# Delta tiles as pairs of 512 and 256 columns, with a gate tile behind every second one

## The chip, the cores and the metric

The kernel runs on one core of one Trainium2 chip. The metric is the device time of one execution in microseconds (us); the time before is the median of three runs.

## The reference, cut to what matters

Two transformer blocks run one after the other on 256 tokens of width 2048, all in float32. Block 1 normalises x and projects it with one wide matrix `w_in`. The parts of that projection are used as follows:

```
att_qkv, dn_qkv, dn_z, dn_beta, dn_alpha, gate_a, gate_b = split(xn @ w_in)
y_a = neighbourhood_attention(aq, ak, av)                 # 8 heads of 128
q, k, v = split(silu(conv5(dn_qkv)))                      # depthwise, over tokens
y_b = rmsnorm(gated_delta(q, k, v, ...)) * silu(dn_z)     # 8 heads of 128, both directions
mixed = sigmoid(gate_a) * (y_a @ w_proj_a) + sigmoid(gate_b) * (y_b @ w_proj_b)
h = x + mixed @ w_out
h = h + square(relu(rmsnorm(h) @ w_mlp_up)) @ w_mlp_down
```

The gated delta rule solves, per head and chunk of tokens, a unit lower triangular system, in both directions of time. Block 2 (another attention, a gated linear attention and a convolved feed-forward layer) is not touched by the change.

## The kernel before

**Products of one tile.** A weight tile is 2048 x 128 values: 16 slices (k) of 128 x 128. To keep float32 accuracy every operand is split in a high part of type fp32r and a rest: ACT casts the raw weights to `hi` (`split_weights`, L314), DVE subtracts to get `lo` (L233, called at L315). The activations `xa` (tiles A0 to A3) hold high and low part of one k side by side, 256 columns each. `tile_mm` (L368) works one tile off into `acc`, one PSUM bank of 2 x 256 float32 columns, of which there are three. `products` (L338) has two forms. With `one=False` each k has a product of 512 columns (hi by both parts of x, into both halves of acc) and one of 256 columns (lo by the high part, into the first half). The two halves are added later by `total` (L443): a copy on ACT (L446) and an addition on DVE (L448). With `one=True` each k has three products of 256 columns, all into the first half, and nothing is left to add.

**Weights.** `plan` is the list of all weight tiles in their order of use, `want` (L290) appends to it. `emit_split` (L322) takes the next one: SP fetches it into one of three raw buffers, ACT and DVE split it into two pieces of 8 slices, of which four pairs of buffers exist, so two tiles.

**Delta tiles.** `heads_project` (L688) with `dn_post` (L720) works off 12 tiles of four heads: 4 of q, 4 of k, 4 of v. For each, `conv_silu` (L674) scales acc by the tokens' norm into `pre`, convolves (one ACT pass, four DVE passes) and gates with a tanh. The first two tiles of all are computed side by side by `two_mm` (L427) and wait in `spare`; for these alone `two` is true and the halves are added. The other 22 (10 in the first group of heads, 12 in the second) use `one=True`.

**Gate tiles.** `gates` (L1019) works off tiles of gate_b (to the DRAM tensor `gbd`) or gate_a (`gad`): `one=False`, `total`, a multiplication, a tanh.

**Background work and its planner.** After a group's 12 delta tiles, `block1_mix` appends `dn_chain` (L731) to the list `bg`: norms, decays and products per head (the steps with `qku` and `kkm`), four transposes on DVE (L813), 31 substitution steps of two DVE instructions each (L819, L821), then copies on ACT, small products on PE that complete the inverses, and `dn_head` (L876) per head. The chain is a generator: each `yield` names a cost in us, or, negative, a number of slices to hold. `pump` (L477) runs after every fourth slice of a product; it adds `rate` / 4 to `credit` (at most 2.2) and lets the first generator of `bg` run while the credit is positive, at most two steps a call. `rate` is `DNR` = 0.7 in a delta tile and `SPARE` = 2.2 in a gate tile and in an attention tile. `finish` (L508) issues all that is left of a generator at once, and its costs are taken off the credit all the same.

**The order of stages.** `block1_mix` (L1028) issues: the delta tiles of group 0; 16 tiles of gate_b and 4 of gate_a (`GA`), beside which chain 0 runs; the delta tiles of group 1; the last 12 tiles of gate_a, beside which chain 1 begins; then, for the attention, 8 tiles (q and k of heads 0 to 3) and one wide product (v), `finish(dn[1])`, 8 tiles (heads 4 to 7), and the chains `na_chain` (L995) of the two groups. The delta q and k of group 1 lie in the tiles M2 and M3, and the attention's q and k of its second group go to M2 and M3 again, so these wait until chain 1 has read them. Last come 8 tiles of z, then `finish()`, then w_proj_a. Group, chain and head numbers below count from 0.

**What sets the order on an engine.** Within this text order the framework places an instruction on its engine's queue as soon as its operands and buffers are there and nothing earlier in the text is ready; the engine's queue itself is fixed when the program is built.

Of the kernel before, what the change touches and what calls it, by code (L numbers as in the profile page):

```python
# [18 lines left out]
KT = D // P  # L19
# [4 lines left out]
SPARE = 2.2  # L24
# [7 lines left out]
GA = 4  # L32
# [142 lines left out]
class Net:  # L175
# [544 lines left out]
    def dn_post(self, j, h, qk, v):  # L720
        v, stage = v
        self.rate = DNR
        two = bool(self.spare)
        acc = self.tile_mm(self.xa, one=True)
        y, th = self.conv_silu(acc, 8 * j + h, two)
        if j < 2:
            self.stt(qk[:, j], th, 1.0, y, ALU.add, ALU.mult)
        else:
            self.stt(stage, th, 1.0, y, ALU.add, ALU.mult)

    def dn_chain(self, g, qk, vt, stage):  # L731
        nc = self.nc
# [285 lines left out]

    def gates(self, d, a, b):  # L1019
        st = self.b4("B3", F32, (P, 8, T))  # L1020
        self.rate = SPARE
        for m in range(a, b):
            z = self.evac(self.tile_mm(self.xa), "cy")
            self.act(st[:, m % 8], z, AF.Tanh, scale=0.5)
            if m % 4 == 3:
                self.nc.gpsimd.dma_start(d[:, m - 3:m + 1], st[:, m % 8 - 3:m % 8 + 1])

    def block1_mix(self):  # L1028
        nc = self.nc
        heads = lambda g, b, n: [self.want("w_in", b + 8 * j + 4 * g, 4) for j in range(n)]  # L1030
        heads(0, 16, 3)
        self.want("w_in", 64, 16)
        self.want("w_in", 48, GA)
        heads(1, 16, 3)
        self.want("w_in", 48 + GA, 16 - GA)
        heads(0, 0, 2)
        self.want_chunk(self.I["w_in_v"])
        heads(1, 0, 2)
        self.want("w_in", 40, 8)
        self.want("w_proj_a", 0, 16, 0, 8)  # L1040
        self.want("w_proj_b", 0, 16, 0, 8)
        self.want_wide("w_out")

        gbd = self.dram.tile([P, KT, T], F32, name="gbd")
        gad = self.dram.tile([P, KT, T], F32, name="gad")
        accs = self.setup()
        self.first_two(self.xa)
        vs = self.b4("H1", F32, (P, 2, 512))
        gr = self.tmp([P, 2, 32], "rr", bufs=1)
        for t in range(2):  # L1050
            r = self.rT[:, t:t + 1]
            self.act(gr[:, t], accs[t][:, 0:32], AF.Copy, scale=r)
            self.act(vs[:, t, 0:240], accs[t][:, 32:272], AF.Copy, scale=r)
            self.act(vs[:, t, 240:512], accs[2 + t][:, 0:272], AF.Copy, scale=r)
        self.vd = [self.dram.tile([P, 2, 512], F32, name="vd%d" % i) for i in range(2)]
        nc.gpsimd.dma_start(self.vd[0], vs)
        self.bg.append(self.dn_gates(gr))
        self.oT = [self.b4("H0")]
        dn = []
        for g in range(2):  # L1060
            stage = self.b4("H1" if g else "H3")
            qk, vt = self.heads_project(g, self.dn_post, stage)
            dn.append(self.dn_chain(g, qk, vt, stage))
            self.bg.append(dn[-1])
            if g == 0:
                self.gates(gbd, 0, KT)
            self.gates(gad, GA * g, KT if g else GA)
        ya = []
        na = []
        for g in range(2):  # L1070
            self.finish(dn[g])
            qk, vt = self.heads_project(g, self.na_post)
            if g == 0:
                tag = "B3"
            else:
                self.finish(dn[1])
                tag = "B2"
            self.ya = ya = ya + self.acts(tag)
            na.append(self.na_chain(g, qk, vt))
            self.bg.append(na[-1])  # L1080
        self.finish(dn[1])
        yb = self.acts("B0", "B1")

        self.rate = 1.2
        for h in range(8):
            z = self.evac(self.tile_mm(self.xa), "cy")
            th = self.tmp([P, T], "th")
            self.act(th, z, AF.Tanh, scale=0.5)
            self.stt(z, th, 1.0, z, ALU.add, ALU.mult)
            o = self.oT[h // 4][:, h % 4]  # L1090
            self.tt(z, o, z, ALU.mult)
            self.split(yb[h], z)
        self.finish()
        ma = [self.b4("M%d" % i) for i in range(4)]
        for i in range(4):
            nc.gpsimd.dma_start(ma[i], gad[:, 4 * i:4 * i + 4])
        mb = [self.b4("H%d" % i) for i in range(4)]
        for i in range(4):
            nc.gpsimd.dma_start(mb[i], gbd[:, 4 * i:4 * i + 4])
        for m in range(KT):  # L1100
            a = ma[m // 4][:, m % 4]
            self.stt(a, a, 1.0, self.total(self.tile_mm(self.ya)), ALU.add, ALU.mult)
        mx = self.actsA()
        for m in range(KT):
            b = mb[m // 4][:, m % 4]
            self.stt(b, b, 1.0, self.total(self.tile_mm(yb, m == 15)), ALU.add, ALU.mult)
            self.tt(b, b, ma[m // 4][:, m % 4], ALU.add)
            self.split(mx[m], b)
        return mx
# [480 lines left out]
```

## Time and profile before

| | us |
|---|---|
| median of 3 runs (2564.48 to 2567.22) | 2566.35 |
| the profiled execution, whole | 2567.14 |
| its span, first to last instruction | 2565.3 |
| PE busy | 2549.0 (99%) |
| PE weight loads busy | 2210.4 (86%) |
| DVE busy | 1762.0 (69%) |
| ACT busy | 1368.6 (53%) |

A matmul record overlaps the next one, since products are pipelined, so the distance between two starts is what one costs; a busy PE is not a PE at its peak. The granted clock of TensorE is 1.00 (2.4 GHz) in every stretch that is used below.

### The profile page before, as it was taken

Reading aid. Unit: us, or ns where it says so; the run is one execution under the profiler, and the core shown is the slowest. Engines: PE = TensorE matmul, PEld = TensorE weight load, DVE = VectorE, ACT = ScalarE, POOL = GpSimd, SP = SyncE. Lnnn points to the kernel's source line nnn. Section 1 sums busy time; section 2 is a strip of 40 time slices with the busy share of each in tenths; the row PEclk is TensorE's granted clock in tenths of the full one; section 3 lists DMA queues with packets and bytes.
Section 4 is the critical chain, followed back from the end, with each engine's and each line's share of the span. In section 5 each row is a group of like instructions: output and inputs, shape, how many; then the busy total and the mean of one; then the engine's idle time right before and its main releaser. Section 6 shows DMA issues by size and latency. Waiting matters only on the chain.

```text
span 2565.3 us, 37124 instructions
## 1 busy us (share of the span) xinstructions
PE 2549.0 (99%) x14386; PEld 2210.4 (86%) x14386; DVE 1762.0 (69%) x2953; ACT 1368.6 (53%) x2277; POOL 49.6 (2%) x102
## 2 busy tenths in 40 slices
PE   8999999999999999999999999999999999999999
PEld 8989988888888888888888888888888888888887
DVE  7887879477856556556556677676688658875884
ACT  6555664665555435445445566655555445543553
POOL 0010000000000000000000000000000000000000
PEclk9999999999999999999999999999999999999999
DMA  7565455455755555555555564445555555555554
GB/s 266 184 214 205 165 197 198 149 200 188 255 182 190 188 196 190 189 196 188 191 196 186 189 216 162 147 165 183 182 194 188 190 197 186 192 195 187 193 190 155
DMA packets 76832, 488.82 MB, mean 191 GB/s; under 512 B 9080, under 2 KB 9368, under 8 KB 24433
## 3 DMA queue, kind: packets, MB, share of 16 engines
q1 hardware_dynamic: 68112, 457.34, 50.2%
q0 software_dynamic: 8256, 28.55, 3.4%
q8 instruction: 113, 1.85, 0.3%
q10 hardware_dynamic: 288, 0.57, 0.1%
q14 instruction: 63, 0.51, 0.1%
HBM read 476.95 MB, written 9.47 MB: 190 GB/s over the span
## 4 chain that ended last, share of the span: by engine, by line
PE 82%; DVE 2%; issue 1%; ACT 1%; DMA 0%; POOL 0%; ACTq 0%; POOLq 0%
PE acc L248 62%; PE s L248 20%; PE s L251 1%; DVE lo L233 0%; DVE rsu L233 0%; DMA rB<-rd 0%; DMA A<-in_c_dram 0%; ACT hi L314 0%; ACT big L245 0%; DVE rsr L236 0%; DVE M L233 0%; DVE sc L236 0%; DVE B L236 0%; ACT B L832 0%; DVE ea L233 0%
## 5 line engine op out<-in xcount | busy, mean ns | idle before, releaser
L233 DVE TENSOR_TENSOR lo<-raw,hi 128x1024 fp32r<-128x1024 f32 (+3 forms) x880 | 1060.3, 1206 | 693.8 <-ACT hi L314 690.7
L314 ACT CAST hi<-raw 128x1024 fp32r<-128x1024 f32 (+3 forms) x880 | 912.1, 1037 | 1014.2 <-PE acc L248 652.6
L248 PE MATMUL acc<-B,hi 128*128 128x512 f32 x2944 | 1028.6, 393 | 0.0
L248 PE MATMUL acc<-B,lo 128*128 128x256 f32 x2944 | 825.7, 280 | 0.0
L248 PEld LDWEIGHTS acc<-B,hi 128*128 128x128 f32 x2944 | 551.1, 187 | 121.6
L248 PEld LDWEIGHTS acc<-B,lo 128*128 128x128 f32 x2944 | 556.4, 189 | 0.3
L248 PE MATMUL acc<-A,hi 128*128 128x512 f32 (+1 forms) x1632 | 463.3, 352 | 0.0
L248 PE MATMUL s<-hi,A 128*128 128x512 f32 (+1 forms) x1280 | 384.2, 381 | 7.6 <-ACT hi L314 7.6
L248 PE MATMUL acc<-hi,A 128*128 128x512 f32 x1152 | 362.7, 390 | 0.0
L248 PE MATMUL acc<-A,lo 128*128 128x256 f32 x1280 | 359.5, 281 | 0.0
L248 PEld LDWEIGHTS acc<-A,hi 128*128 128x128 f32 x1632 | 283.6, 189 | 38.9 <-issue 0.2
L248 PEld LDWEIGHTS s<-hi,A 128*128 128x128 f32 x1280 | 235.6, 189 | 52.8 <-ACT hi L314 7.6
L248 PEld LDWEIGHTS acc<-hi,A 128*128 128x128 f32 x1152 | 216.2, 188 | 44.9
L248 PEld LDWEIGHTS acc<-A,lo 128*128 128x128 f32 x1280 | 242.5, 189 | 0.8
L248 PE MATMUL s<-lo,A 128*128 128x512 f32 (+1 forms) x640 | 238.6, 381 | 0.7 <-DVE lo L233 0.6
L248 PE MATMUL acc<-lo,A 128*128 128x512 f32 x576 | 224.2, 389 | 0.1
L248 PEld LDWEIGHTS s<-lo,A 128*128 128x128 f32 x640 | 118.7, 189 | 23.7 <-DVE lo L233 1.3
L236 DVE SCALAR_TENSOR_TENSOR cy<-pre,par,cy 128x256 f32<-128x256 f32 x272 | 130.5, 482 | 5.4 <-ACT cy L245 0.6
L248 PEld LDWEIGHTS acc<-lo,A 128*128 128x128 f32 x576 | 108.1, 188 | 22.6 <-DVE lo L233 0.5
L233 DVE TENSOR_TENSOR ea<-acc,eb 128x256 f32<-128x256 f32 x258 | 107.7, 418 | 0.8 <-ACT eb L446 0.8
L446 ACT COPY eb<-acc 128x256 f32<-128x256 f32 x258 | 93.4, 363 | 0.0
L248 PE MATMUL acc<-hi,B 128*128 128x512 f32 (+2 forms) x192 | 68.7, 369 | 0.0
(284 smaller groups left out, 1647.2 us busy)
## 6 DMA issues: line engine op xcount, KB each, us to landing
raw<-in_w_in_dram SPq DMA_DIRECT2D x112, 1024.0 KB, 4.8
raw<-in_w_up_dram SPq DMA_DIRECT2D x88, 1024.0 KB, 4.8
raw<-in_w_mlp_up_dram SPq DMA_DIRECT2D x64, 1024.0 KB, 4.8
raw<-in_w_mlp_down_dram SPq DMA_DIRECT2D x64, 1024.0 KB, 4.6
raw<-in_w_down_dram SPq DMA_DIRECT2D x44, 1024.0 KB, 4.6
raw<-in_w_out_dram SPq DMA_DIRECT2D x32, 1024.0 KB, 4.7
raw<-in_w_proj_a_dram SPq DMA_DIRECT2D x16, 512.0 KB, 3.5
raw<-in_w_proj_b_dram SPq DMA_DIRECT2D x16, 512.0 KB, 3.4
```

Of the source, the lines that this page charges most:

```text
L233: return (eng or self.nc.vector).tensor_tensor(out=out, in0=a, in1=b, op=op).ins
L236: self.nc.vector.scalar_tensor_tensor(out=out, in0=a, scalar=s, in1=b, op0=op0, op1=op1)
L248: self.nc.tensor.matmul(out, lhsT, rhs, start=start, stop=stop)
L251: self.nc.tensor.transpose(out, a, self.ident[0:a.shape[0], 0:a.shape[0]])
L314: self.nc.scalar.copy(hi, w)
L446: self.nc.scalar.copy(t, acc[0:np_, 1])
```

## The change

Delta tiles take the other form of product (512 and 256 columns for each slice) and add their halves as all others do. `gates` becomes a generator that works off one tile a step; `dn_post` takes a step of it behind every second delta tile. Six gate tiles of a group so lie between its delta tiles, and the other ten follow behind them, after the group's chain has been appended. Group 0 now has all 16 tiles of gate_b, group 1 all 16 of gate_a. The list of weights is put in the same order.

```diff
     def dn_post(self, j, h, qk, v):
         v, stage = v
         self.rate = DNR
-        two = bool(self.spare)
-        acc = self.tile_mm(self.xa, one=True)
-        y, th = self.conv_silu(acc, 8 * j + h, two)
+        acc = self.tile_mm(self.xa)
+        y, th = self.conv_silu(acc, 8 * j + h, True)
         if j < 2:
             self.stt(qk[:, j], th, 1.0, y, ALU.add, ALU.mult)
         else:
             self.stt(stage, th, 1.0, y, ALU.add, ALU.mult)
+        if h % 2 == 1:
+            next(self.between)
...
     def gates(self, d, a, b):
         st = self.b4("B3", F32, (P, 8, T))
-        self.rate = SPARE
         for m in range(a, b):
+            self.rate = SPARE
             z = self.evac(self.tile_mm(self.xa), "cy")
             self.act(st[:, m % 8], z, AF.Tanh, scale=0.5)
             if m % 4 == 3:
                 self.nc.gpsimd.dma_start(d[:, m - 3:m + 1], st[:, m % 8 - 3:m % 8 + 1])
+            yield
...
-        heads(0, 16, 3)
-        self.want("w_in", 64, 16)
-        self.want("w_in", 48, GA)
-        heads(1, 16, 3)
-        self.want("w_in", 48 + GA, 16 - GA)
+        for g, m in ((0, 64), (1, 48)):
+            for j in range(6):
+                self.want("w_in", 16 + 8 * (j // 2) + 4 * g + 2 * (j % 2), 2)
+                self.want("w_in", m + j, 1)
+            self.want("w_in", m + 6, 10)
...
             stage = self.b4("H1" if g else "H3")
+            self.between = self.gates(gad if g else gbd, 0, KT)
             qk, vt = self.heads_project(g, self.dn_post, stage)
             dn.append(self.dn_chain(g, qk, vt, stage))
             self.bg.append(dn[-1])
-            if g == 0:
-                self.gates(gbd, 0, KT)
-            self.gates(gad, GA * g, KT if g else GA)
+            for i in self.between:
+                pass
```

## Rows read from the trace of the kernel before

**Rows 1.** Page, part 1: busy us, share and instructions of each engine.

```profile
PE 2549.0 (99%) x14386; PEld 2210.4 (86%) x14386; DVE 1762.0 (69%) x2953; ACT 1368.6 (53%) x2277; POOL 49.6 (2%) x102
```

**Rows 2.** Page, part 4: the chain that ended last, by engine.

```profile
PE 82%; DVE 2%; issue 1%; ACT 1%; DMA 0%; POOL 0%; ACTq 0%; POOLq 0%
```

**Rows 3.** Windows: us, busy us (instructions) of engines; clock, DMA share, GB/s.

```profile
47.00:108.30 61.30, 61.18 (x509) 60.44 (x508) 56.01 (x128) 36.12 (x64) 2.71 (x5) 1.00 0.62 207
...
397.00:441.40 44.40, 44.40 (x258) 38.83 (x257) 42.70 (x96) 18.45 (x25) 0.68 (x2) 1.00 0.55 197
441.40:472.60 31.20, 31.07 (x322) 24.74 (x321) 14.97 (x16) 19.99 (x35) 1.53 (x4) 1.00 0.48 170
472.60:598.00 125.40, 124.74 (x749) 109.47 (x747) 84.93 (x212) 81.77 (x193) 9.04 (x16) 1.00 0.49 171
```

**Rows 4.** Timeline, PE: start, us; two successive delta tiles' first products.

```profile
59.36 0.40 PE L248 MATMUL acc<-A,hi 128*128 128x256 f32 x2
...
65.12 0.40 PE L248 MATMUL acc<-A,hi 128*128 128x256 f32 x2
```

**Rows 5.** Timeline, PE: first products of two pairs of successive gate tiles.

```profile
129.68 0.40 PE L248 MATMUL acc<-A,hi 128*128 128x512 f32 x1
...
135.32 0.40 PE L248 MATMUL acc<-A,hi 128*128 128x512 f32 x1
...
183.79 0.39 PE L248 MATMUL acc<-A,hi 128*128 128x512 f32 x1
...
189.34 0.39 PE L248 MATMUL acc<-A,hi 128*128 128x512 f32 x1
```

**Rows 6.** Page, part 5: group, count; busy us, mean ns; idle before, releaser.

```profile
L233 DVE TENSOR_TENSOR lo<-raw,hi 128x1024 fp32r<-128x1024 f32 (+3 forms) x880 | 1060.3, 1206 | 693.8 <-ACT hi L314 690.7
...
L236 DVE SCALAR_TENSOR_TENSOR cy<-pre,par,cy 128x256 f32<-128x256 f32 x272 | 130.5, 482 | 5.4 <-ACT cy L245 0.6
L233 DVE TENSOR_TENSOR ea<-acc,eb 128x256 f32<-128x256 f32 x258 | 107.7, 418 | 0.8 <-ACT eb L446 0.8
L446 ACT COPY eb<-acc 128x256 f32<-128x256 f32 x258 | 93.4, 363 | 0.0
```

**Rows 7.** Groups by line, window 20 to 400: the chain's transposes and substitution.

```profile
L813 DVE STREAM_TRANSPOSE B<-B 32x1024 f32<-32x1024 f32 x6 | 12.2, 2028 | 0.1
...
L233 DVE TENSOR_TENSOR B<-B,prod 128x126 f32<-128x126 f32 (+22 forms) x31 | 7.9, 255 | 0.8
```

**Rows 8.** Timeline, DVE and PE: last substitution, wide product, first inverse, first heads.

```profile
441.18 0.18 DVE L233 TENSOR_TENSOR B<-B,prod 128x16 f32<-128x16 f32 x1
...
441.43 0.39 PE L248 MATMUL acc<-hi,A 128*128 128x512 f32 x1
...
451.50 1.19 PE L248 MATMUL s<-big,B 32*32 32x32 f32 x32
...
472.60 0.60 PE L251 MATMUL s<-ident,M 128*128 128x128 f32 x4
...
479.25 0.68 PE L248 MATMUL s<-S,M 128*128 128x128 f32 x4
```

**Rows 9.** Groups by line, window 472 to 598: the attention chains' products on PE.

```profile
L248 PE MATMUL s<-M 128*128 128x256 f32 x32 | 8.7, 378 | 0.0
...
L248 PE MATMUL s<-big,H 128*128 128x256 f32 x32 | 7.7, 382 | 0.0
...
L251 PE MATMUL s<-ident,sc 128*128 128x128 f32 x32 | 4.4, 274 | 0.0
```

**Rows 10.** Tile bi, loads: ns min/median/max, first and last start us.

```profile
L1002 POOL DMA_DIRECT2D bi<-in_bias_dram x8: 539/540/567, 3.8 to 562.4; - x8
```

**Rows 11.** Timeline of POOL: the attention's v for group 0.

```profile
310.73 1.50 POOL L698 DMA_DIRECT2D H<-vd  x2 [39.29 <-ACT th L245]
```

**Rows 12.** Tile sc, window 505 to 605: exponentials of the attention, ns.

```profile
L245 ACT ACTIVATE sc<-sc,smx x16: 492/502/513, 516.6 to 592.5; 128x256 f32<-128x256 f32 x16
```

**Rows 13.** Waits of PE, 47 to 600: us in total, times, longest.

```profile
PE s L251 <- ACT rA L245: 0.7, 2, 0.5
```

## The prediction

> **What bounds the kernel.** I begin with the page's engine table: PE is busy 99% of the span [rows 1], and the chain that ended last is PE's for 82% [rows 2]. A stage is worth what it does to PE's queue. The windows by stage come next [rows 3]: in the delta tiles of group 0 (47 to 108.3) PE has no idle time worth naming and DVE is busy 56.0 of 61.3 us; while the last substitution runs (397 to 441.4) DVE is busy 42.7 of 44.4 us and PE still does not wait; in the wide product behind it (441.4 to 472.6) DVE has more than half its time free. Then the timeline of PE, for what a tile costs. From 47 to 600 PE's largest waits come to 0.7 us each [rows 13], so the change can win only by cheaper products, and lose only by new waits.
>
> **The products.** A delta tile takes 65.12 - 59.36 = 5.76 us [rows 4], a gate tile, which already has the pair form, 5.55 or 5.64 us (189.34 - 183.79, 135.32 - 129.68 [rows 5]). 22 delta tiles change form, so between 22 x 0.12 = 2.6 and 22 x 0.21 = 4.6 us go. I take 0.18 (most gate tiles run at the lower figure): 4.0 us.
> The Trainium skill ("TensorE: Matmul & The Clock Gate", section Back-to-back issue gap) gives the isolated warm distance of two products as N / 2.4 + 2.5 ns. By it three of 256 columns and a pair of 512 and 256 differ by one fixed 2.5 ns a slice: 352 slices, 0.9 us, and the sum below would be 3.1 us higher. The rows disagree (0.12 to 0.21 us a tile is 8 to 13 ns a slice); since both forms stand in this trace, the measurement decides and the rule gets no chance of its own.
>
> **What is added.** 22 copies of 0.363 us on ACT and 22 additions of 0.418 us on DVE [rows 6], 9.2 us of DVE. A delta tile then costs DVE two splits, four convolution passes of 0.482 us and three further passes: 2 x 1.21 + 1.93 + 3 x 0.42 = 5.6 us by durations, about PE's 5.55. The gate tile behind every second one needs 2 x 1.21 + 2 x 0.42 = 3.3. Three tiles: 14.5 us of DVE beside 16.7 of PE. Without the gates in between DVE would set the pace; with them the splits, which may run two tiles ahead, stay ahead. In group 0, where no chain runs, I cost this at nothing. In group 1 chain 0 runs beside it with 0.7 + 0.7 + 2.2 = 3.6 of credit in three tiles: 18.1 against 16.7, over six such triples 8 us too much. What gives is the chain, whose steps depend on each other (0.255 us each [rows 7]), so that a ready split gets in between any two; PE's cover is that look-ahead of two tiles. I take 0, with 8 us as the other end. The moved gate tiles keep their eight stores on POOL (busy 2% of the span [rows 1]) and SP's loads only change their order, one tile for another of the same size: nothing.
>
> **What is moved: the chains.** This is the part that costs. Chain 0 is appended behind group 0's delta tiles in both kernels, but six gate tiles of that group are now used up before it exists, and their credit with them. Up to the end of group 1's delta tiles: before 20 x 2.2 + 12 x 0.7 = 52.4, after 10 x 2.2 + 12 x 0.7 + 6 x 2.2 = 43.6; with the gates behind them 78.8 and 65.6. Chain 1, which waits in `bg` behind chain 0, is therefore 13.2 later, six gate tiles' worth. Before, its last substitution ends just as the wide product starts (441.18 and 441.43 [rows 8]). Counting the yields forward, in the changed kernel three transposes and all 31 substitution steps are open at that point; the wide product's 16 slices grant 8.8, and `finish(dn[1])` issues the last 21 steps, the inverses and all heads at once.
> What that does to PE: 3 x 2.03 + 31 x 0.51 = 21.9 us of DVE [rows 7] are open at the wide product's start. Without the inverses this product takes 96 x 0.231 = 22.2 us (0.231 is two thirds of 5.55 / 16); DVE was busy 15.0 us there [rows 3], so some 7 us go into the chain, and 15 remain at its end, X. From the last substitution to M2's release took, before, 10.3 (441.18 to 451.50) + 21.1 (to 472.60) + 7.3 us (to the last read of q and k by the first pair of heads, 479.25 + 0.68) = 38.7 [rows 8], the middle part paced by slices of the wide product: its PE work is only 31.2 - 22.2 = 9.0. Unpaced I take 7 + 12 + 7.3 = 26, nearer to the bare work; bounds 21 and 38.7. M2 is free at X + 41 (36 to 54).
> The next attention tiles write M2 and M3. The first of these writes is DVE's; behind it wait the fourth attention tile on PE, for an acc buffer, and the later splits on DVE. Three tiles fit in the three acc buffers, 16.7 us; beside them PE's queue has the inverses (9.0), half of the heads' 7.3 us (4) and no further tile. 41 - 29.7 = 11 us are open, between 6 and 24.
> What can fill them: the products of attention group 0, whose operands lie ready since before the wide product. Half of 8.7 + 7.7 + 4.4 is 10.4 us of PE [rows 9]. Their text stands much later, but the queues do look ahead: the attention's biases are loaded from 3.8 us on [rows 10], and v of group 0 at 310.73, while delta group 1 still runs [rows 11]. So I leave 3 us of the 11 bare. The debt of credit then keeps attention group 1 back until the final `finish`: 36 steps there in place of 8. Its 10.4 us of PE lie beside exponentials and scalings on ACT (two of each in a head, 0.50 us [rows 12], 8 us for four heads, and the copies); first tiles of w_proj_a can begin on the heads that are done. Bare: 0 to 8, I take 2.
> A product that waits holds what is queued behind it: for a transpose of a head PE stood idle twice, 0.7 us in total, with tiles left to do [rows 13]. The Trainium skill ("PSUM — Partial Sum Buffer", section Engine vs sequencer instructions) says the same, that matmuls start and complete in program order; by that rule alone, no attention product counting as queued ahead, the time would be rival 1's.
>
> **Sum.** 2567.1 (profiled execution: span 2565.3 and 1.8 around it) - 4.0 + 3 + 2 = 2568.1. The profiled execution lies 0.8 above the median of the runs, so 2567.4 for the median.
>
> **Rivals.**
> 1. The gap is not filled: the attention's products stay behind the z tiles in PE's queue. Place: the first tiles of attention group 1. Price 11, and at the final `finish` nearly seven heads in place of four, 3. 2566.35 - 4.0 + 14 = 2576. It decides from the point at which M2 comes free later than X + 30. For it: the order of a queue is fixed when the program is built, and PE does stand idle behind a waiting product [rows 13]. Against it: rows 10 and 11.
> 2. DVE-bound in group 1: 6 of the 8 us too much reach PE in the delta tiles themselves. With the waits of the likeliest case 2567.4 + 6 = 2573. For it: DVE at 42.7 of 44.4 us in 397 to 441 [rows 3]. Against: PE did not wait there.
> 3. No new wait, only the products' gain: 2566.35 - 4.0 = 2562.4. For it: so few waits in the whole trace before.
> 4. A real gain: all 22 tiles at 4.6 and the old waits gone as well: 2566.35 - 4.6 - 1.5 = 2560.3. The trace has little more to give.
>
> **Chances.** Likeliest (2564 to 2571) 0.47; rival 1 0.28; rival 2 0.05; rival 3 0.13; rival 4 0.07. What a measurement of this kernel can tell from no change is 0.2%, 5.1 us: faster is below 2561.2, slower above 2571.5. So faster 0.07, same 0.47 + 0.13 = 0.60, slower 0.28 + 0.05 = 0.33. The range leaves out rival 4 and the worst of rival 1: 2561.5 to 2578.
>
> **What would show it.** A delta tile of 5.55 to 5.64 us on PE; in group 1's delta tiles a DVE without idle time and a substitution that reaches into the gates behind them; chain 1's last substitution after the wide product rather than before it; then either attention products of group 0 between the inverses and heads, or an idle PE of about 11 us before the first write of M2. PE idle in the delta tiles would be rival 2. I am wrong altogether if chain 1 ends as early as before, or if PE idles by more than 15 us in one place.

## The result, and the profile after

The changed kernel takes 2588.16 us in the median of 6 runs (2583.14 to 2590.94), the kernel before 2566.78 in 6 runs beside it. The ratio is 1.0082, with a 95% interval of 1.0072 to 1.0092: 21.4 us slower. The forecast was 2567.4, within 2561.5 to 2578. The profiled execution took 2585.37 us (span 2583.6), 18.2 more than the one before.

Part 1 of the page of the changed kernel, answering to [rows 1]:

```profile
PE 2554.1 (99%) x14034; PEld 2196.5 (85%) x14034; DVE 1768.4 (68%) x2975; ACT 1373.4 (53%) x2299; POOL 49.3 (2%) x102
```

Its part 4, answering to [rows 2]:

```profile
PE 89%; issue 4%; DVE 4%; ACT 1%; DMA 1%; POOL 0%; SPq 0%; ACTq 0%; DVEq 0%; POOLq 0%
```

352 instructions fewer on PE, and PE is busy longer by 5.1 us: some products must have become slower. The windows by stage show where. They answer to [rows 3] (us, busy us of PE, PEld, DVE, ACT, POOL, then the granted clock, and what DMA did). The first line is the second group's delta tiles with the gates between them, then the wide product, chain 1's inverses and heads, the final forced end, and the whole stretch from the first delta tile into w_proj_a:

```profile
203.00:303.00 100.00, 100.00 (x579) 88.19 (x578) 95.92 (x193) 56.32 (x97) 2.15 (x4) 1.00 0.57 199
...
437.00:459.00 22.00, 22.00 (x99) 18.18 (x99) 21.27 (x37) 9.21 (x10) 0.54 (x1) 1.00 0.53 184
459.00:525.00 66.00, 60.07 (x541) 52.58 (x540) 40.71 (x121) 39.95 (x106) 4.26 (x8) 0.95 0.38 128
...
583.00:622.00 39.00, 32.59 (x140) 25.30 (x138) 18.99 (x68) 22.35 (x61) 5.37 (x10) 0.87 0.39 130
...
47.00:700.00 653.00, 637.25 (x4017) 555.42 (x4018) 496.63 (x1061) 375.53 (x751) 37.07 (x69) 0.99 0.55 188
```

The kernel before, over the same tiles (18 us fewer) and in the 39 us that hold its own final end:

```profile
47.00:682.00 635.00, 632.66 (x4375) 568.63 (x4374) 491.51 (x1043) 370.94 (x732) 37.11 (x69) 1.00 0.56 194
583.00:622.00 39.00, 39.00 (x223) 33.75 (x222) 29.62 (x55) 22.23 (x43) 1.60 (x3) 1.00 0.60 203
```

PE stood idle for 653.00 - 637.25 = 15.8 us after the change, for 2.3 before: 13.4 us more. And the granted clock, 1.00 in both stretches before, is 0.95 and 0.87 in two stages. Cut finer, it is 0.50 (1.2 GHz) in four stretches:

```profile
479.70:486.50 6.80, 4.95 (x43) 4.16 (x45) 2.17 (x4) 6.33 (x15) 0.30 (x1) 0.50 0.31 129
595.80:599.20 3.40, 3.40 (x10) 2.69 (x9) 0.87 (x3) 0.74 (x2) 0.53 (x1) 0.50 0.02 5
606.00:609.40 3.40, 3.40 (x10) 2.68 (x9) 0.73 (x2) 0.74 (x2) 0.00 (x0) 0.50 0.01 6
616.30:619.70 3.40, 3.40 (x10) 2.77 (x9) 0.66 (x2) 0.75 (x2) 0.38 (x1) 0.50 0.00 0
```

That is 17.0 us at half speed. PE was busy for 15.1 of them, so some 7.6 us of work were left undone (the rest is idle time, counted above). PE's waits from 47 to 640 us (total, times, longest), answering to [rows 13], say where it stood:

```profile
PE s L248 <- DVE big L825: 5.2, 1, 5.2
PE s L251 <- ACT sc L975: 4.7, 5, 1.2
PE acc L248 <- DVE ea L233: 1.8, 1, 1.8
PE s L251 <- ACT rA L245: 1.2, 3, 0.6
PE s L248 <- ACT B L843: 1.1, 1, 1.1
PE s L248 <- ACT big L987: 1.0, 4, 0.3
```

The first is chain 1. The timeline of DVE (start, us), answering to [rows 8], has its last substitution step at 478.52, where it was 441.18, and the second of the two transposes behind it at 480.79:

```profile
478.52 0.17 DVE L233 TENSOR_TENSOR B<-B,prod 128x16 f32<-128x16 f32 x1
478.73 1.07 DVE L824 STREAM_TRANSPOSE B<-B 128x512 f32<-128x512 f32 x1
479.69 1.19 DVE L233 TENSOR_TENSOR lo<-raw,hi 128x1024 fp32r<-128x1024 f32 x1
480.79 0.71 DVE L825 STREAM_TRANSPOSE big<-B 128x512 f32<-128x512 f32 x1
```

PE's timeline shows the first product of the fourth attention tile behind the wide product, and then nothing for 5.25 us. What it waits for is the second of those transposes, an operand of the inverses:

```profile
475.92 0.39 PE L248 MATMUL acc<-A,hi 128*128 128x512 f32 x1
481.56 1.64 PE L248 MATMUL s<-big,B 32*32 32x32 f32 x27 [5.25 <-DVE big L825]
```

The other waits are the final forced end, that is, what the last `finish()` issues in a row: four pairs of attention heads, 583 to 622 us. Two rows from its first and second pair, and the whole attention's scaling on DVE (first and last start), which begins at 568.0 only:

```profile
585.23 0.55 PE L251 MATMUL s<-ident,sc 128*128 128x128 f32 x3 [1.18 <-ACT sc L975]
...
593.90 0.94 PE L251 MATMUL s<-ident,sc 128*128 128x128 f32 x6 [1.05 <-ACT sc L975]
```

```profile
L236 DVE SCALAR_TENSOR_TENSOR sc<-s,bi x16: 414/418/425, 568.0 to 611.5; 128x256 f32<-128x256 f32 x16
```

The products did what was forecast. First products of two delta tiles and of the gate tile behind them, answering to [rows 4]: 5.54 and 5.55 us for a delta tile, 5.76 before, and no wait.

```profile
208.21 0.39 PE L248 MATMUL acc<-A,hi 128*128 128x512 f32 x1
...
213.75 0.39 PE L248 MATMUL acc<-A,hi 128*128 128x512 f32 x1
...
219.30 0.39 PE L248 MATMUL acc<-A,hi 128*128 128x512 f32 x1
```

**The account.** Products 22 x 0.21: -4.6. Idle PE: +13.4. Half clock: +7.6. Sum +16.4 of the 18.2 us between the two profiled executions; 1.8 us stay unexplained.

### The profile page after: what moved, and what is told of

It is laid out like the page before. It is cut to its first block, busy times and chain, and to the rows that moved or that the text cites. A ratio compares the mean times of both kernels' runs of the same rounds, so it can differ in the third digit from the quotient of the medians.

```text
span 2583.6 us, 36525 instructions
## 1 busy us (share of the span) xinstructions
PE 2554.1 (99%) x14034; PEld 2196.5 (85%) x14034; DVE 1768.4 (68%) x2975; ACT 1373.4 (53%) x2299; POOL 49.3 (2%) x102
## 4 chain that ended last, share of the span: by engine, by line
PE 89%; issue 4%; DVE 4%; ACT 1%; DMA 1%; POOL 0%; SPq 0%; ACTq 0%; DVEq 0%; POOLq 0%
PE acc L248 67%; PE s L248 21%; DVE lo L233 1%; PE s L251 1%; DMA raw<-in_w_in_s_dram 0%; ACT hi L314 0%; DVE cy L236 0%; DVE rsu L233 0%; ACT sc L245 0%; DMA rB<-rd 0%; DMA A<-in_c_dram 0%; DVE ea L233 0%; ACT sc L975 0%; DVE smx L965 0%; DVE sc L236 0%
## 5 line engine op out<-in xcount | busy, mean ns | idle before, releaser
L248 PE MATMUL acc<-A,hi 128*128 128x512 f32 x1280 | 457.7, 400 | 0.0
L248 PEld LDWEIGHTS acc<-A,hi 128*128 128x128 f32 x1280 | 240.6, 188 | 52.4 <-issue 0.2
L233 DVE TENSOR_TENSOR ea<-acc,eb 128x256 f32<-128x256 f32 x280 | 116.9, 418 | 1.3 <-ACT eb L446 1.3
L446 ACT COPY eb<-acc 128x256 f32<-128x256 f32 x280 | 101.0, 362 | 2.1 <-PE acc L248 2.1
L245 ACT ACTIVATE cy<-pre,par 128x256 f32<-128x256 f32 x112 | 64.7, 579 | 17.7 <-DVE pre L233 17.1
```

The costliest lines, as they stand in the source:

```text
L233: return (eng or self.nc.vector).tensor_tensor(out=out, in0=a, in1=b, op=op).ins
L245: self.nc.scalar.activation(out, a, f, **k)
L248: self.nc.tensor.matmul(out, lhsT, rhs, start=start, stop=stop)
L446: self.nc.scalar.copy(t, acc[0:np_, 1])
```

## The experiments

Ratios are against the kernel before, run on the same chip in the same rounds. Where a mean clock of a run is named, it is the granted clock over the whole span. A step is what a chain issues from one `yield` to the next; a step is forced when a `finish` issues it and not `pump`. The planner is in debt while `credit` is below zero, as it is after a `finish`: until tiles have paid it back, `pump` issues nothing.

**1 and 2. The two halves of the change.** The pairs in the old order:

```diff
-        two = bool(self.spare)
-        acc = self.tile_mm(self.xa, one=True)
-        y, th = self.conv_silu(acc, 8 * j + h, two)
+        acc = self.tile_mm(self.xa)
+        y, th = self.conv_silu(acc, 8 * j + h, True)
```

> Pairs of 512 and 256 columns in the delta tiles, with the order of the kernel before (all gates behind the delta tiles). My theory, that the order alone costs and the pairs gain, expects the products' gain and no more: 22 tiles from 5.76 to 5.55 us, so 4.6 us below before, about 2562, PE without new waits and no fall of the granted clock. The rival, that DVE sets the pace of delta tiles without gates in between (5.6 us of DVE a tile, worked out, against 5.55 of PE), expects PE waits on lo or acc in the delta tiles, 1 to 4 us in group 0 and more in group 1 where chain 0 runs beside: 2563 to 2570.

Measured: 2562.94 us (11 runs), ratio 0.9984 (0.9975 to 0.9993), faster by 4.0 us. In the delta tiles of group 0 (us, busy us of PE, PEld, DVE, ACT) PE hardly waits and DVE still has room:

```profile
47.00:108.00 61.00, 60.88 (x355) 52.79 (x354) 55.62 (x131) 38.68 (x73) 2.71 (x5) 1.00 0.58 201
```

The other half is the changed kernel with that edit undone, so the new order with three products of 256 columns.

> The order of the changed kernel (a gate tile behind every second delta tile), with the three products of 256 columns and no added halves. My theory, that the order by itself makes chain 1 late, whatever the products: before plus 21.4 and the products' 4.6, about 2592, with the PE wait for the substitution near 480 us, the final row of head pairs, and granted clock 0.5 behind them. The rival, that the added 9.2 us of copies and additions on DVE are what delay the chain: the wait of 5.2 us and its clock dip (3.4 us) go, about 2583 or less.

Measured: 2592.68 us (4 runs), ratio 1.0101 (1.0088 to 1.0114). Its first two waits on PE:

```profile
PE s L248 <- DVE big L826: 4.9, 1, 4.9
PE s L251 <- ACT sc L976: 4.7, 5, 1.2
```

The halves add up: -4.0 and +25.7 make +21.7, and +21.4 was measured. The order alone costs, and of the added 9.2 us of DVE work no cost shows: without them the wait is 4.9 us in place of 5.2, and the rival's 2583 is missed by 10.

**3. The lateness without the order.** The pairs in the old order, and when chain 1 is appended the planner is put into debt:

```diff
+DEBT = 19.0
...
             self.bg.append(dn[-1])
+            self.credit -= DEBT * g
```

> Pairs in all delta tiles in the order of the kernel before, and a debt of 19 us put on the planner when chain 1 is appended. By the yields this leaves forced what the changed kernel leaves forced: 21 substitution steps, then 61 attention steps at the final end (25 and 36). Nothing is reordered. If the late chain is the whole cost of the change, this is as slow as the changed kernel: 2585 to 2591, with the wait for the substitution, four pairs of heads in a row at the end and granted clock 0.5 behind both. If the order of the tiles costs something by itself, it stays nearer to the pairs alone, 2563 to 2575.

Measured: 2586.38 us (4 runs), ratio 1.0083 (1.0069 to 1.0097), that of the changed kernel. Its three longest waits on PE are the changed kernel's:

```profile
PE s L249 <- DVE big L824: 5.2, 1, 5.2
PE s L252 <- ACT sc L974: 4.7, 5, 1.2
PE acc L249 <- DVE ea L234: 1.8, 1, 1.8
```

The last substitution step starts at 478.07 us, 478.52 in the changed kernel. The clock was at 0.50 for 13.7 us from 478.6 on and for 3.4 us from 615.1 on. So the late chain is enough for the whole cost, to within the 2 us between the two medians, and nothing is left for the order of the tiles by itself. The debt that does it is 19, not the 13.2 us of credit that the prediction counted as lost. In the traces the lag is longer too: chain 1's first transpose stood 46.8 us ahead of the wide product before (394.63 to 441.43) and stands 1.1 ahead of it now (436.05 to 437.17). That is 45.7 us, eight tiles of 5.55 us and not six.

**4 to 6. The two places.** The debt struck out behind chain 1's forced end (the line stands behind chain 0's `finish` too), and more rate beside the z tiles, so that no attention step is left to the final end:

```diff
             self.finish(dn[g])
+            self.credit = 0.0
...
-        self.rate = 1.2
+        self.rate = 2.2
         for h in range(8):
             z = self.evac(self.tile_mm(self.xa), "cy")
```

> The changed kernel, with the planner's debt struck out after chain 1's forced end (credit set to 0) and rate 2.2 in place of 1.2 in the z tiles, so that no attention step is left to the final forced end; chain 1 stays as late as it is. My theory: the wait near 480 us and its dip of the clock stay (5.2 + 3.4 us), the 7.7 us of idle and the three half-clock stretches of 3.4 us (5.1 us) at the final forced end go: about 2588 - 12.8 = 2575. The rival, that the attention heads cost PE the same waits wherever they stand: about 2588.

Measured: 2579.6 us (6 runs, 2570.48 to 2583.20), ratio 1.0044 (1.0030 to 1.0058); 2574.3 in the profiled execution. The final end's waits are gone, the wait for the substitution is as it was:

```profile
PE s L248 <- DVE big L825: 5.3, 1, 5.3
PE s L251 <- ACT rA L245: 1.3, 3, 0.6
```

The runs lie 12.7 us apart, those of the pairs alone 4.0. The lowest had a mean clock of 0.999, the highest 0.993: six thousandths of 2572 us are 15 us. The mechanism held. The median is 4.6 us above the forecast, and the runs line up by their mean clocks; where it fell in the others is not known. In the profiled one it fell for 6.8 us at the substitution and for 3.4 us at 312, behind a wait of 1.16 us that the changed kernel has too (1.14 at 307.5), there without a fall.

Then the attention heads of group 0 issued in turn with chain 1's forced end:

```diff
-            self.finish(dn[g])
+            if g:
+                self.bg = [self.side_by_side([dn[1], na[0]])]
+                self.finish(self.bg[0])
+            self.finish(dn[g])
```

> The changed kernel; at chain 1's forced end the steps of attention group 0 are issued in turn with it, one of each, where they stood behind it before. This does by hand what my prediction assumed that the queues would do. If attention group 0 can fill the wait for the substitution, the idle 5.2 us near 480 us and the 3.4 us that the clock cost behind it go, and the final forced end has four heads in place of eight (half of 7.7 us of idle and of 5.1 us of clock): 2588 - 8.6 - 6.4 = 2573. The rival, that the heads' work on DVE (a scaling, a maximum and small ones for each of 8 parts) makes the substitution itself later by as much, expects the wait to stay: about 2582, the final end's half alone.

Measured: 2585.29 us (5 runs), ratio 1.0067 (1.0055 to 1.0080). The longest wait is now this:

```profile
PE s L251 <- ACT sc L975: 6.4, 3, 4.1
```

4.08 of these 6.4 us stand at 467.1, a little ahead of the inverses: the heads' transposes wait for their exponentials, and the products behind them wait too. One wait took the other's place, and the last substitution step came later as well (486.62), which is the rival's part. The clock was 0.50 for 3.4 us behind the wait and for 17.1 us from 496.2 on, among the inverses' small products and the heads' transposes; in the 16 us ahead of that PE had waited for 0.7 us only. My theory fell: put there in turn, one step of each, the attention does not fill that gap. With the debt struck out as well:

> As the run with attention group 0 issued beside chain 1's forced end, and then the planner's debt struck out and rate 2.2 in the z tiles, so that attention group 1 has its steps beside the z tiles. If the two places, wait and final end, are all that the late chain costs, this ends at the time of the pairs in the old order plus what is left of small waits: 2563 to 2568. If a chain this late costs more than these, above 2570.

Measured: 2573.74 us (7 runs), ratio 1.0035 (1.0022 to 1.0048), with the 4.08 us wait still there (at 469.5), half clock for 3.4 us behind it and for 6.8 us at 312.7. So a chain this late costs more than the two places: 10.8 us over the pairs alone.

**7 to 9. The credit given back.** More rate in the gate tiles behind a chain, in the changed kernel:

```diff
-            self.rate = SPARE
+            self.rate = SPARE if m < 6 else 3.6
```

> The changed kernel, with the planner's rate 3.6 in place of 2.2 in the gate tiles behind a chain (20 tiles by 1.4 us, 28 us of credit; 13.2 were lost). By the yields chain 1's last substitution step is then issued in the wide product, as before, only 5 of the inverses' 6 parts and the heads are left to the forced end, and attention group 0 starts in the fifth attention tile of group 1. My theory, that lost credit is the whole cost: no wait for the substitution, 11 forced attention steps in place of 61, and a time of 2562 to 2567. The rival, that DVE has no room for a faster chain: PE waits in the gate tiles or the delta tiles of group 1 instead, 2570 or more.

Measured: 2573.74 us (5 runs), ratio 1.0037 (1.0024 to 1.0050). The wait for the substitution and the long final end are gone, but:

```profile
PE acc L248 <- DVE lo L233: 2.3, 1, 2.3
PE s L248 <- ACT B L843: 2.2, 1, 2.2
```

The first is a split that came late in group 1's delta tiles: from 195 to 210 us DVE was busy 14.86 of 15 us, with two of chain 0's transposes (4.01 us) right ahead of that split. DVE has no room there for a faster chain. The second is the inverses, still issued in a row at the forced end; behind it the clock was at 0.50 for 6.8 us. Both theories were half right. Rate 4.0, with the two edits of the debt run:

> The changed kernel with rate 4.0 in the gate tiles behind a chain, the debt struck out and rate 2.2 in the z tiles. By the yields the substitution of chain 1 then begins in the last gate tile and its inverses stand in the wide product as in the kernel before; no attention step is left to the final end. If credit is the whole cause: 2562 to 2566, the waits of the run with rate 3.6 at the inverses (2.2 us) and its dip of the clock gone. If DVE has no room for it, a wait for a split (lo) in the delta tiles of group 1, 2.3 us at rate 3.6, grows, and the time stays at 2568 or more.

Measured: 2580.88 us (6 runs), ratio 1.0050 (1.0037 to 1.0063). The splits are now late three times:

```profile
PE acc L248 <- DVE lo L233: 5.5, 3, 3.3
```

The rival holds, but the splits are not the whole of it. In the wide product, where the inverses stand as in the kernel before, PE waited 0.92 and 0.57 us (until 448.33 and 451.90). Then came the longest stretch at half clock of all traces, some 10 us of work, PE being busy all through it:

```profile
454.30:474.80 20.50, 20.50 (x164) 16.35 (x162) 3.08 (x4) 6.41 (x11) 0.83 (x2) 0.50 0.30 104
```

Gate tiles between the delta tiles of group 1 alone (the loop over `self.between` runs for g = 1, on gate_a from `GA` on; group 0's 20 gate tiles follow its delta tiles):

```diff
+            self.between = self.gates(gad, GA, KT) if g else None
             qk, vt = self.heads_project(g, self.dn_post, stage)
...
-            if g == 0:
-                self.gates(gbd, 0, KT)
-            self.gates(gad, GA * g, KT if g else GA)
+            for i in self.between or self.gates_all(gbd, gad):
+                pass
```

> Pairs in all delta tiles; gate tiles stand between delta tiles in group 1 alone (six of the 12 gate_a tiles), group 0 keeps its 20 gate tiles behind. Chain 0 so has its old credit, chain 1 loses six tiles. By the yields 4 substitution steps are forced in place of 21, and 28 attention steps at the final end in place of 61. My theory: no wait of 5 us for the substitution, half of the final end's cost (12.8 us by 28 / 61 is 5.9): 2563 + 6 = 2569, between 2565 and 2572. A rival, that gate tiles between delta tiles of group 1 are what costs, because chain 0 then runs beside deltas with DVE full: as late as the changed kernel, 2580 or more.

Measured: 2579.23 us (6 runs), ratio 1.0047 (1.0034 to 1.0060). That lies just under the rival's 2580 and 7 us above my range. The substitution ended at 459.1, as the wide product ended, and yet PE waited 5.3 us. DVE's timeline:

```profile
459.09 0.17 DVE L233 TENSOR_TENSOR B<-B,prod 128x16 f32<-128x16 f32 x1
459.30 1.16 DVE L824 STREAM_TRANSPOSE B<-B 128x512 f32<-128x512 f32 x1
...
467.60 0.71 DVE L825 STREAM_TRANSPOSE big<-B 128x512 f32<-128x512 f32 x1 [0.52 <-DMA vd<-big]
```

The second transpose writes a buffer of the tag `big`. Forced past the wide product's end, it stands on DVE's queue behind three splits, and behind the wide product's v, which lies in `big` until its store has landed; the row names that store as its releaser. That the shared buffer sets its place is read from this, not tested. My count of few forced steps was right, that there would be no wait was not.

**10 and 11. Useless work against idle time.** In the changed kernel, four products that nothing reads ahead of each head's transposes in the final end (`self.fill` is 4 there, else 0):

```diff
         pt = self.ps()
+        for i in range(self.fill):
+            self.mmul(pt, self.xa[0][:, 0, 0:P], self.xa[0])
```

> The changed kernel, with four products of 512 columns that nothing reads in front of each attention head's transposes in the final forced end (32 in all, 32 by 0.231 is 7.4 us of useless work for PE, where it stands waiting for the exponentials for 5.7 us). If the clock falls there because PE stands idle, the three half-clock stretches of 3.4 us behind the pairs of heads go (5.1 us), the useless work takes the place of idle time but for 2 us, and the time is no higher than the changed kernel's: about 2585. If the clock falls for another reason (the many small products), the stretches stay and the time is 2590 to 2595.

Measured: 2587.17 us (5 runs), ratio 1.0082 (1.0069 to 1.0095), 1.0 us below the changed kernel and within the runs' spread, 2 us above the forecast. In its trace (us, busy us, then the clock) the final end is as forecast, with PE busy and the clock whole (until 625.2, where it fell for 3.4 us behind the last wait, of 1.8 us):

```profile
583.00:622.00 39.00, 38.22 (x198) 31.73 (x198) 22.52 (x75) 25.38 (x69) 6.44 (x12) 1.00 0.52 162
481.80:495.40 13.60, 11.13 (x129) 9.56 (x129) 3.64 (x4) 8.62 (x20) 0.65 (x3) 0.50 0.39 149
75.60:79.00 3.40, 3.40 (x11) 2.92 (x12) 3.03 (x9) 0.42 (x1) 0.52 (x1) 0.50 0.15 53
```

But the same execution lost elsewhere: 13.6 us at half clock at the wait for the substitution, 6.8 in the changed kernel's trace; 3.4 at 311.1, behind a wait of 0.89; and 3.4 at 75.6, where PE had not waited but had worked off 22 small products in the 3 us before. So the idle heads can account for the falls in the final end, but it is one execution: with the same idle heads the clock fell three times there in the changed kernel and once in experiment 3. And the added products are large, so they fill the waits and thin out the small products at once; which of the two keeps the clock up stays open. That filling them saves time is not shown.

And 22 such products ahead of the third attention tile's own, in front of the wait for the substitution (`self.pad` is 22 there, else 0):

```diff
+        for i in range(self.pad):
+            self.mmul(acc, pieces[0][0][:, 0], X[0], start=True, stop=True)
         for hi, lo, m in pieces:
```

> The changed kernel, with 22 products of 512 columns that nothing keeps (5.1 us) in front of the third attention tile of group 1, ahead of the wait for the substitution. If PE waits there because it has no other work, the extra work takes the wait's place: wait 0 to 1 us, no clock 0.5 near 480 us, and a time 3 us below the changed kernel, 2585. If PE waits because the inverse stands at a fixed place of its queue, and the framework put it there by its own idea of when the chain is ready, the inverse now stands before more of the attention products, the wait stays at 5 to 6 us with its dip, and the extra work is paid in full or nearly: 2589 to 2593.

Measured: 2591.00 us (4 runs), ratio 1.0099 (1.0086 to 1.0113), 2.8 above the changed kernel:

```profile
PE s L249 <- DVE big L828: 5.4, 1, 5.4
```

The wait did not shrink by a tenth of a microsecond. Only 32 slices of attention tiles stood before the inverse in place of 48; the rest had moved behind it. So PE waits there not for want of work, but because the inverse has its place in the queue some 5 us ahead of the chain; with 5.1 us of work added, 16 other slices stood behind it instead. That the framework, when it built the queue, took the chain for shorter than it is on the chip is my reading of this; it is argued, not shown.

**12. What is left to win.** Experiment 1 with rate 2.2 beside the z tiles:

> Pairs in the order of the kernel before, with the planner's rate 2.2 in place of 1.2 in the z tiles: the 8 attention steps that are left to the final forced end there go too. The pairs alone wait 2.5 us on PE between 46 and 700 us, 0.6 of it at that end. If these waits are all there is to win: 2562.3, within 1 us of the pairs alone; more DVE and ACT work beside the z tiles could make PE wait there: 2565.

Measured: 2563.81 us (11 runs), ratio 0.9988 (0.9979 to 0.9997): no gain over the pairs alone; at the final end PE's wait is 1.6 us in place of 0.6. The pairs in the old order are the version that beats both kernels.

## Why the prediction was wrong

| term, profiled execution | predicted us | measured us |
|---|---|---|
| products of 22 delta tiles | -4.0 | -4.6 |
| added DVE work | 0 | 0 (experiments 1 and 2) |
| wait for chain 1 | +3 | +5.25 |
| final end, idle PE | +2 | +7.5 |
| other waits | 0 | +0.7 |
| TensorE's clock | no term | +7.6 |
| unexplained | 0 | +1.8 |

- **Products, DVE.** Right; the tiles run at the lower figure of [rows 5] throughout. The distance between DVE's 18.1 and PE's 16.7 us in group 1 came out of the chain as forecast: DVE busy 95.9 of 100 us, PE without a wait.
- **Chain 1 late.** Right, and with the open steps that the yields gave (31 at the wide product's start; 20 behind its last product in the trace, 21 forecast). Its end X was forecast 15 us behind the wide product and came 19.6 behind it (478.7 and 459.1). Experiment 3 makes the same lateness without the order and gets the same time.
- **"What can fill them: the products of attention group 0".** This step failed. They came at 568 us. The early loads of biases and of v [rows 10, 11] showed that POOL's queue looks ahead, and I took that for PE too. On PE they stayed where the text has them, among the last z tiles and in the final end. Experiment 5 puts them where I wanted them, and they bring a wait of their own. The place was wrong too: I expected PE to stand before the first write of M2, with 11 us open; it stood ahead of the inverses, 5.25 us bare with nothing in it, and for M2 not at all. Experiment 11 speaks for the queue's order as the reason.
- **The final finish.** I counted 36 steps there. The debt kept back 25 more of group 0, and what I priced at 2 us is four pairs in a row that each wait for exponentials: 7.5 us (1.18 + 0.19 + 0.32 + 3 x 1.05 + 0.28 + 0.27 + 0.28, and 1.79 before w_proj_a). Rival 1 had "nearly seven heads", and 3 us.
- **The clock.** No term stood for it in the sum or in any rival, since the trace before shows 1.00 everywhere. It was the largest single miss. Each run's time less its share of lost clock (1 - mean clock, times its span) is an estimate of the time at full clock (to a us or two, as the clock is recorded in thousandths): for the changed kernel 2575 to 2583, median 2577. That is next to rival 1's 2576, by luck: its 11 + 3 us of waits were 5.25 + 7.5, one too large and one too small. By this estimate the other 11 us of the median's 2588 are the clock. The Trainium skill ("TensorE: Matmul & The Clock Gate", section HAM oscillation — how this bites in real kernels) tells of a kernel whose engine falls to half clock behind each of its waits, and counts half of the time spent there as lost. The traces here agree with that price where PE is busy: in experiment 8 products of 512 columns start 0.43 us apart at 0.50 (461.66 to 462.09) and 0.23 at 1.00 (475.15 to 475.38).
- **Chances.** Rival 1, no filling of the gap, had 0.28 and came nearest in mechanism. The range ended at 2578, ahead of rival 1's worst; with 11 us for the clock that end would have been 2589.

## What to carry to other kernels

Where background work is paced by a budget, count the budget that a reordering takes from it, and where its remainder will be forced out: a chain issued in one row has no slack, and here PE waited 4.9 to 5.4 us for it in all seven versions that left it to the `finish` alone. Price a new wait on TensorE at its length plus half of PE's busy time at half clock that follows, and look at the granted clock by stage even where the trace before shows none of it. Test the two halves of a change apart: here the useful half was worth 4.0 us, and the other cost 25.7.

## What the runs showed of the hardware

In nine traces PE stood idle for 4.1 to 5.4 us ahead of the inverses (or of the heads put there). In all nine the granted clock was 0.50 in a stretch that began while PE stood or just after, and lasted between 3.4 us (experiments 5 and 6) and 13.7 us (experiments 3 and 10). Behind waits of about 1 us among small products it fell in some executions and not in others, at the same place: 3.4 us at 312 in experiment 4, none in the changed kernel. Waits of 2.35 and 3.31 us for splits, between tiles of large products (experiments 7 and 8), were followed by none. And it fell where PE had hardly waited: for 20.5 us in experiment 8 and 17.1 us in experiment 5, both among the inverses' small products, and for 3.4 us at 75.6 in experiment 10. So idle time is not the only thing that went before a fall: small products without a wait did too. For the waits of about 1 us, which have small products around them, no run separates the two. Runs of one kernel spread with the clock: 12.7 us in experiment 4, where the time rises as the mean clock sinks from 0.999 to 0.993, against 4.0 for the pairs alone, whose mean clock was 1.000 in all 11 runs.

What the useful half saves can be put per product. The new form has the same columns for a slice (768) and one product less, and a tile costs 0.21 us less over 16 slices: 13 ns for a product beyond its columns. With that, 5.55 us for 32 products and 12288 columns leaves 0.418 ns a column, and a product of 512 columns should cost 0.227 us. The wide product starts its 96 products of 512 columns from 437.17 to 458.74 us, 0.227 apart. This is an estimate from these three rows.
